# Where the filler stands beside the attention: first scores, changes of head, first scan products

## The chip, the cores and the metric

The kernel runs on one core of a Trainium2 chip, as one launch. The metric is the device time of that launch in microseconds, as the median of three runs. The core has five engines with a queue each: TensorE (PE; its weight loads are shown apart as PEld), VectorE (DVE), ScalarE (ACT), GpSimd (POOL) and SyncE (SP). SP computes nothing here; it issues nearly all the DMAs.

## The reference

One block of a diffusion backbone: 1024 latent tokens and 256 context tokens, width 1024, float32. What matters for the change is the token mixer, whose two halves don't depend on each other:

```python
hl = modulate(rmsnorm(xl, norm1_g), ...)        # (1024, 1024)
zl, xbcl, dtl, ql, kl, vl = split(hl @ w_in)    # one input projection
# attention half: 4 heads, two softmax maps each, over 256 + 1024 keys
w   = softmax(q1 k1) - lam * softmax(q2 k2)
o_l = rmsnorm(w @ v, subln_g) * (1 - lam_init)
# scan half: 16 heads in chunks of 128, forward and backward
ys_l = rmsnorm(ssd_bidir(xbcl, dtl, ...) * silu(zl), ssd_norm_g)
yl   = concat([ys_l, o_l]);  xl = xl + gate * (yl @ w_out)
```

Behind it come a gated feed-forward part with a convolution and a last norm, which the change doesn't touch.

## The kernel before, in words

The program goes through stages: start-up, input projection (`inproj`), the attention with filler, the rest of the scan, and `mixffn` (head norm, output projection, feed-forward). The change lies in the attention stage.

`attention` is a generator over 32 query tiles of 128 queries, n = 0 to 31, eight to a head. For each tile there are two groups of scores (c = 0 and 1, the two softmax maps): six products into one PSUM buffer `sc` of 1280 columns, which has no second copy, then the row maximum on DVE (`stat`), the exponential on ACT (`et`). `weigh` joins the two maps of the tile before on DVE, `transpose` brings the result into place in ten transposes (`tr`), and after every second tile `values` makes the product with V (`po`). In heads 0 and 1 the transposed weights are split into a high and a low part, in heads 2 and 3 not. At each new head `load_head` issues on SP's queue the loads of queries `S`, keys `K` (two maps, two parts, each twice) and values `V`; S and K have one buffer for each map and part in use, so that the new head's loads wait until the old head's last scores are through.

Where TensorE would wait, the generator yields a gap, a number in about microseconds, and `run` fills it: it adds `fill * gap` to a debt and takes steps from a second generator, the filler, until their stated costs have paid the debt. The filler is first `zproj`, the gate projection: eight units of weights, two halves of 512 tokens each, eight steps to a half, and each step three products `pz` at a cost of 0.65; behind each half come `zo` on ACT and DVE and a store to `zt`. When that is used up, the second `run` takes `ssd`, the scan: nine backward and two forward state steps (`s`, cost 3.4, with `xw` and `hb` or `H` multiplied on POOL), then eight chunks of outputs (`scs`, `yo`, `y`, `yt`), each with two halves, and seven more forward states. TensorE keeps the order in which all this is written (`pin`). What is left of the scan after the last tile runs beside the head norm (`cs_ps`, `cr_ps`, `bc_ps`), and then the output projection begins with the products `pw`. DMAs stand in SP's queue in one order, and one that waits holds up those behind it.

Of the kernel before, what the change touches and what calls it, by code (L numbers as in the profile page):

```python
# [75 lines left out]
E_S4 = "gvvv"  # L76
E_T4 = "vgvv"
E_W = "ggv"
FIRST_GAP = 12.0
S_BUFS = 6  # L80
D_BLOCKS = 3, 3, 3, 2
D_PLAIN = 2
# [13 lines left out]
B_FILL = 1.1  # L96
# [3 lines left out]
def r32(ap):  # L100
    return ap.bitcast(F32)


class Prog:
# [145 lines left out]
    def build(self):  # L250
        with ExitStack() as es:
            self.consts(es)
            hw, att, ssd = ExitStack(), ExitStack(), ExitStack()
            self.startup(hw)
            with ExitStack() as e:
                self.inproj(e, hw)
            e_pm, e_pa = ExitStack(), ExitStack()
            self.pm = self.pool(e_pm, "pm", 3, space=PSUM)
            self.pa = self.pool(e_pa, "pa", 2, space=PSUM)
            self.pin, self.rest = True, False  # L260
            at = self.attention(att)
            z = self.zproj(hw)
            self.run(at, z, A_FILL, False)
            hw.close()
            sd = self.ssd(ssd)
            self.run(at, sd, B_FILL, True)
            self.pin = False
            att.close()
            e_pa.close()

            def ssd_rest():
                self.rest = True
                for _ in sd:
                    pass
                ssd.close()

            with ExitStack() as e:
                self.mixffn(e, ssd_rest, e_pm)

    def run(self, at, filler, fill, drain):  # L280

        debt = 0.0
        for tile_no, gap in at:
            debt += fill * gap
            while debt > 0:
                cost = next(filler, None)
                if cost is None:
                    if not drain:
                        return
                    break  # L290
                debt -= cost
# [485 lines left out]
    def attention(self, es):  # L777

        nc = self.nc
        ap = self.pool(es, "ap", 2)  # L780
        heads = {}

        def load_head(h):
            pair, hh = divmod(h, 2)
            S, K = [], []
            for c in range(2):
                hc = 2 * hh + c
                s = ap.tile([P, SEQ], F32R, name="S")
                nc.sync.dma_start(r32(s), r32(self.qd[pair, hc].rearrange("a b r t -> (a b r) t")))
                k2 = []  # L790
                for part in range(2):
                    kt = ap.tile([P, TOK], F32R, name=f"K{part}")
                    for dup in range(2):
                        nc.sync.dma_start(r32(kt[dup * 64:(dup + 1) * 64, :]),
                                          r32(self.kd[pair, hc, part].rearrange("b r t -> (b r) t")))
                    k2.append(kt)
                S.append(s), K.append(k2)
            v = []
            for s in range(1 if h >= F32_FROM else 2):
                vt = ap.tile([P, NT, VD], F32R, name=f"V{s}")  # L800
                nc.sync.dma_start(r32(vt), r32(self.vd[h, s]))
                v.append(vt)
            return S, K, v

        def scores(n, c, st):
            h, qt = divmod(n, NL)
            S, K, _ = heads[h]
            sc = self.pa.tile([P, TOK], F32, tag="sc", name="sc", bufs=1)
            for o, w in ((0, 512), (512, 512), (1024, 256)):
                for i in range(2):  # L810
                    self.mm(sc[:, o:o + w], S[c][:, qt * P:(qt + 1) * P], K[c][i][:, o:o + w], i == 0, i == 1)
            et = ap.tile([P, TOK], F32, name="et", bufs=3)
            acc = self.s0[:, qt, h:h + 1] if c == 0 else st[:, 4:5]
            nc.vector.tensor_reduce(out=st[:, c:c + 1], in_=sc, axis=AX.X, op=ALU.max, negate=True)  # L814
            nc.scalar.activation(et, sc, AF.Exp, bias=st[:, c:c + 1], accum_out=acc)  # L815
            return et

        def weigh(n, st, ex):
            h, qt = divmod(n, NL)
            nc.vector.reciprocal(out=st[:, 5:6], in_=st[:, 4:5])  # L820
            nc.vector.scalar_tensor_tensor(out=st[:, 6:7], in0=st[:, 5:6], scalar=self.nlam[:, 0:1],
                                           in1=self.s0[:, qt, h:h + 1], op0=ALU.mult, op1=ALU.mult)
            nc.vector.scalar_tensor_tensor(out=ex[0], in0=ex[1], scalar=st[:, 6:7], in1=ex[0], op0=ALU.mult, op1=ALU.add)
            return ex[0]

        def transpose(n, w, wt, gi):
            m = 4 if gi < 2 else 2
            tr = self.pa.tile([P, 4, P], F32, tag="tr", name="tr")
            for i in range(m):
                kt = gi * 4 + i  # L830
                self.pe(nc.tensor.transpose(tr[:, i, :], w[:, kt * P:(kt + 1) * P], self.ident))
            qi = n % 2
            hi, lo = (t[:, :m, qi * P:(qi + 1) * P] for t in wt[gi])
            if n // NL >= F32_FROM:
                (nc.scalar.copy if WT_ENG[gi] == "a" else nc.vector.tensor_copy)(r32(hi), tr[:, :m, :])
            else:
                self.split(hi, lo, tr[:, :m, :])

        def values(n, wt):
            h, qt = divmod(n, NL)  # L840
            v = heads[h][2]
            po = self.pa.tile([P, 512], F32, tag="tr", name="po")
            for kt in range(NT):
                g, i = divmod(kt, 4)
                if h >= F32_FROM:
                    self.mm(po[:, :256], r32(v[0][:, kt, :]), r32(wt[g][0][:, i, :]), kt == 0, kt == NT - 1)
                    continue
                self.mm3(po[:, :256], (v[0][:, kt, :], v[1][:, kt, :]), (wt[g][0][:, i, :], wt[g][1][:, i, :]),
                         kt == 0, kt == NT - 1)
            oo = ap.tile([P, 256], F32, name="oo")  # L850
            nc.scalar.copy(oo, po[:, :256])
            nc.sync.dma_start(self.od[h][:, (qt - 1) * P:(qt + 1) * P], oo)

        n_all = DA_H * NL
        wt, done, prev = None, None, None
        for n in range(n_all + 2):
            if n < n_all:
                if n % NL == 0:
                    heads[n // NL] = load_head(n // NL)
                if n == 0:  # L860
                    yield n, FIRST_GAP
                st = ap.tile([P, 8], F32, name="stat", bufs=4)
                e0 = scores(n, 0, st)
            if done is not None:
                values(*done)
                done = None
                long = False
            else:
                long = True
                yield n, G_LONG if n < n_all else 2.0  # L870
            if prev is not None:
                m, pst, pex = prev
                w = weigh(m, pst, pex)
            if n < n_all:
                e1 = scores(n, 1, st)
            if prev is not None:
                if m % 2 == 0:
                    wt = [[ap.tile([P, 4, 256], F32R, name=f"wt{s}", bufs=4) for s in range(2)] for _ in range(3)]
                for gi in range(2):
                    transpose(m, w, wt, gi)  # L880
                yield n, G_A if long else G_B
                transpose(m, w, wt, 2)
                if m % 2 == 1:
                    done = (m, wt)
                yield n, G_A if long else G_B
            prev = (n, st, [e0, e1]) if n < n_all else None
# [749 lines left out]
```

## Time and profile before

| | before |
|---|---|
| median of three runs | 1842.23 us (1840.81 to 1844.36) |
| profiled execution, own time | 1847.34 us |
| its span | 1845.6 us |
| mean granted TensorE clock | 0.947 |
| PE, PEld, DVE, ACT, POOL busy | 87%, 69%, 67%, 41%, 59% of the span |
| first gate product to first product of the output projection | 430 to 909 us |

Times inside the program are microseconds from the start of the span. The busy shares are means over stages with different limits; products are pipelined, so that a busy PE isn't PE at its peak.

### The profile page before, as it was taken

To read this page: it belongs to the slowest core of one execution; us is meant where nothing else is said; L and a number is where in the kernel's file an instruction comes from. 1 tells how busy PE (TensorE), PEld (TensorE's weight loads), DVE (VectorE), ACT (ScalarE), POOL (GpSimd) and SP (SyncE) were. 2 spreads that over 40 slices of the span, in tenths; PEclk is the share of its full clock that TensorE was granted. 3 is DMA by queue.
4 is the path that set the end of the run, shared out by engine and by line. 5 is a ranking of instruction groups with operands and counts; after the bars stand their busy time and mean duration, and the time that the engine had idled before them with its cause. 6 is when DMAs were issued, how large, how long until landed. Compare 5 with 4: busy or idle time off the path is not lost.

```text
span 1845.6 us, 21271 instructions
## 1 busy us (share of the span) xinstructions
PE 1614.2 (87%) x7588; PEld 1274.8 (69%) x7588; DVE 1241.7 (67%) x1432; ACT 754.8 (41%) x1400; POOL 1096.5 (59%) x720
## 2 busy tenths in 40 slices
PE   5989989997899878898898967899999998989976
PEld 2687777885678656766577756677777776767755
DVE  4469843353556576887854686766767667898886
ACT  4433577632444333444443553233333334344242
POOL 3341587783010054677556768777887887777751
PEclk8899999998999998999999988899999999999988
DMA  7356766767241566546453312322222234743222
GB/s 270 126 183 207 266 205 231 250 216 206 100 120 44 144 221 190 173 152 213 135 202 120 121 45 74 108 86 86 97 90 100 86 106 166 265 162 126 63 78 91
DMA packets 138826, 273.35 MB, mean 148 GB/s; under 512 B 11984, under 2 KB 60544, under 8 KB 138208
## 3 DMA queue, kind: packets, MB, share of 16 engines
q1 hardware_dynamic: 138128, 271.03, 44.3%
q8 instruction: 60, 0.98, 0.2%
q0 software_dynamic: 592, 0.96, 0.2%
q14 instruction: 46, 0.38, 0.1%
HBM read 197.63 MB, written 74.32 MB: 147 GB/s over the span
## 4 chain that ended last, share of the span: by engine, by line
PE 37%; DVE 20%; POOL 18%; DMA 11%; issue 9%; ACT 4%; SPq 0%; POOLq 0%; DVEq 0%; ACTq 0%
PE pu L145 8%; POOL wlo L126 6%; PE pd L145 6%; POOL S L1206 4%; PE lat L145 4%; PE pz L145 3%; PE sc L145 3%; PE pb L145 3%; DMA K<-kd 3%; PE pw L145 3%; DVE T L126 2%; DMA gd<-R 2%; DMA wt<-wmB 2%; DVE jk L523 2%; PE pv L145 1%
## 5 line engine op out<-in xcount | busy, mean ns | idle before, releaser
L145 PE MATMUL pu<-T,whi 128*128 128x512 f32 x1232 | 389.9, 397 | 10.6 <-ACT whi L125 10.6
L145 PE MATMUL pu<-T,wlo 128*128 128x512 f32 x616 | 249.5, 405 | 38.6 <-POOL wlo L126 30.9
L145 PEld LDWEIGHTS pu<-T,whi 128*128 128x128 f32 x1232 | 236.9, 192 | 61.2 <-ACT whi L125 11.7
L126 POOL TENSOR_TENSOR wlo<-wraw,whi 128x512 fp32r<-128x512 f32 (+2 forms) x118 | 164.7, 1400 | 96.6 <-ACT whi L125 88.5
L145 PE MATMUL lat<-hl,w_hi 128*128 128x512 f32 x640 | 206.4, 399 | 5.0 <-DVE dtt L599 3.8
L145 PE MATMUL pd<-T,whi 128*128 128x512 f32 x560 | 182.3, 406 | 14.5 <-DVE T L126 8.1
L126 POOL TENSOR_TENSOR w_lo<-w_raw,w_hi 128x1024 fp32r<-128x1024 f32 (+1 forms) x36 | 83.7, 2328 | 184.6 <-ACT w_hi L125 162.9
L126 POOL TENSOR_TENSOR wlo<-S,whi 128x512 fp32r<-128x512 f32 (+2 forms) x122 | 169.0, 1395 | 27.0 <-ACT whi L125 26.7
L145 PEld LDWEIGHTS pu<-T,wlo 128*128 128x128 f32 x616 | 118.4, 192 | 80.0 <-POOL wlo L126 43.5
L814 DVE TENSOR_REDUCE stat<-sc 128x1 f32<-128x1280 f32 x64 | 95.3, 1488 | 109.1 <-PE sc L145 109.0
L125 ACT CAST whi<-wraw 128x512 fp32r<-128x512 f32 (+2 forms) x140 | 81.2, 581 | 194.9 <-PE pu L145 110.5
L145 PEld LDWEIGHTS lat<-hl,w_hi 128*128 128x128 f32 x640 | 123.0, 193 | 30.9 <-DVE dtt L599 4.0
L145 PE MATMUL sc<-K,S 128*128 128x512 f32 (+1 forms) x384 | 98.9, 395 | 49.5 <-DMA K<-kd 25.1
L125 ACT CAST whi<-S 128x512 fp32r<-128x512 f32 (+2 forms) x144 | 81.6, 571 | 147.6 <-PE pu L145 94.7
L815 ACT ACTIVATE et<-sc,stat 128x1280 f32<-128x1280 f32 x64 | 85.1, 1330 | 134.7 <-DVE stat L814 116.3
L145 PEld LDWEIGHTS pd<-T,whi 128*128 128x128 f32 x560 | 108.7, 196 | 43.9 <-DVE T L126 13.3
L145 PE MATMUL pd<-T,wlo 128*128 128x512 f32 x280 | 115.0, 411 | 16.7 <-POOL wlo L126 16.6
L145 PE MATMUL lat<-hl,w_lo 128*128 128x512 f32 x320 | 128.1, 400 | 0.0
L145 PEld LDWEIGHTS sc<-K,S 128*128 128x128 f32 x384 | 74.6, 203 | 77.1 <-ACT et L815 33.6
L538 POOL TENSOR_TENSOR R<-R,never 128x1024 f32<-128x1024 f32 x32 | 80.7, 2537 | 43.6 <-DMA R<-atd 41.6
L542 ACT ACTIVATE R<-R,lna 128x128 f32<-128x128 f32 x256 | 78.2, 391 | 56.0 <-POOL R L538 55.9
L908 POOL TENSOR_TENSOR xw<-xt,dte 128x1024 f32<-128x1024 f32 x18 | 36.9, 2050 | 96.1 <-DMA xt<-xtok 71.7
(283 smaller groups left out, 3729.9 us busy)
## 6 DMA issues: line engine op xcount, KB each, us to landing
wraw<-wUp SPq DMA_DIRECT2D x46, 512.0 KB, 3.3
wt<-wmB SPq DMA_DIRECT2D x32, 512.0 KB, 3.9
R<-atd SPq DMA_DIRECT2D x32, 512.0 KB, 5.5
stg<-gf_d SPq DMA_DIRECT2D x21, 768.0 KB, 4.9
w_raw<-wU SPq DMA_DIRECT2D x28, 512.0 KB, 5.0
gf_d<-T SPq DMA_DIRECT2D x11, 1024.0 KB, 4.2
K<-kd SPq DMA_DIRECT2D x32, 320.0 KB, 7.8
xt<-xtok SPq DMA_DIRECT2D x19, 512.0 KB, 5.2
```

Source lines behind the costliest of these rows:

```text
L125: nc.scalar.copy(hi, src)
L126: (lo_eng or nc.vector).tensor_tensor(out=lo, in0=src, in1=hi, op=ALU.subtract)
L145: self.pe(self.nc.tensor.matmul(out, lhsT=lhsT, rhs=rhs, start=start, stop=stop))
L523: nc.vector.scalar_tensor_tensor(out=jk, in0=wt, scalar=1.0, in1=scb, op0=ALU.mult, op1=ALU.mult, accum_out=self.modl[:, c:c + 1])
L538: nc.gpsimd.tensor_tensor(out=R[:, d], in0=R[:, d], in1=self.never[:, d].unsqueeze(1).broadcast_to([P, 8, P]), op=ALU.add)
L542: nc.scalar.activation(e, e, AF.Exp, bias=self.lna[:, d, i, h:h + 1], scale=1.0)
L814: nc.vector.tensor_reduce(out=st[:, c:c + 1], in_=sc, axis=AX.X, op=ALU.max, negate=True)
L815: nc.scalar.activation(et, sc, AF.Exp, bias=st[:, c:c + 1], accum_out=acc)
L908: nc.gpsimd.tensor_tensor(out=h3(xw), in0=h3(xt), in1=bc_h(self.dte, d, i), op=ALU.mult)
L1206: nc.gpsimd.tensor_tensor(out=t, in0=in0, in1=in1, op=op)
```

## The change

Three constants and the places where they act. The gap ahead of the first scores is 30 instead of 12. At the start of every later head there is a gap of 6, behind the issue of the head's loads and ahead of its first scores. The second `run`, the one with the scan as filler, starts with a debt of -8, so that the first 8 units of `fill * gap` bring no scan step.

```diff
-FIRST_GAP = 12.0
+FIRST_GAP = 30.0
+HEAD_GAP = 6.0
+SD_LAG = 8.0
...
-            self.run(at, sd, B_FILL, True)
+            self.run(at, sd, B_FILL, True, -SD_LAG)
...
-    def run(self, at, filler, fill, drain):
-
-        debt = 0.0
+    def run(self, at, filler, fill, drain, debt=0.0):
+
         for tile_no, gap in at:
             debt += fill * gap
             while debt > 0:
...
                 if n % NL == 0:
                     heads[n // NL] = load_head(n // NL)
-                if n == 0:
-                    yield n, FIRST_GAP
+                    yield n, HEAD_GAP if n else FIRST_GAP
                 st = ap.tile([P, 8], F32, name="stat", bufs=4)
                 e0 = scores(n, 0, st)
```

On TensorE 126 gate products instead of 51 stand ahead of the first scores, 33 instead of 9 between the last transposes of n=7 and the scores of n=8, and the last gate product stands in n=11 instead of n=16. The first state product stands in n=12 instead of n=16, the first chunk of outputs in n=18 instead of n=23. After the last scores (n=31) one chunk is left instead of four.

The first place is the ACT queue around the first exponentials (`et`). Before:

```order
L670 ACTIVATE rhi<-tm_3686 128x512
L772 ACTIVATE zo<-pz 128x512
L125 CAST w_hi<-w_raw 128x1024
L815 ACTIVATE et,s_95<-sc,stat 128x1280
L815 ACTIVATE et,stat<-sc,stat 128x1280
L815 ACTIVATE et,s_95<-sc,stat 128x1280
L772 ACTIVATE zo<-pz 128x512
```

Now:

```order
L671 ACTIVATE rhi<-tm_3686 128x512
L773 ACTIVATE zo<-pz 128x512
L127 CAST w_hi<-w_raw 128x1024
L773 ACTIVATE zo<-pz 128x512
L127 CAST w_hi<-w_raw 128x1024
L773 ACTIVATE zo<-pz 128x512 x2
L816 ACTIVATE et,s_95<-sc,stat 128x1280
```

Three more halves of the gate and the weights of one more unit (`w_hi`) stand ahead of the first exponential.

The second place is SP's queue around the keys of head 2 (`K` from `kd`). Before:

```order
L774 DMA zt<-zo 128x512
L794 DMA K_5242<-kd 64x1280
L789 DMA S<-qd 128x1024
L774 DMA zt<-zo 128x512
L794 DMA K_5242<-kd 64x1280
L794 DMA K_5245<-kd 64x1280 x2
L852 DMA od<-oo 128x256
L794 DMA K_5250<-kd 64x1280
L789 DMA S<-qd 128x1024
L794 DMA K_5250<-kd 64x1280
L794 DMA K_5253<-kd 64x1280 x2
L898 DMA xt<-xtok 128x1024
```

Now (`xt` and `btk` are inputs of a state step, `hbd` takes its result):

```order
L900 DMA btk<-btok 128x256
L795 DMA K_5334<-kd 64x1280
L790 DMA S<-qd 128x1024
L932 DMA hbd<-hb 128x1024
L795 DMA K_5334<-kd 64x1280
L795 DMA K_5337<-kd 64x1280 x2
L898 DMA xt<-xtok 128x1024
L853 DMA od<-oo 128x256
L795 DMA K_5342<-kd 64x1280
L790 DMA S<-qd 128x1024
L795 DMA K_5342<-kd 64x1280
L795 DMA K_5345<-kd 64x1280 x2
```

A store and a load of the scan, which waited behind all keys before, now stand between them.

The third place is the end of the attention, TensorE after the last scores. Before, of which the first rows:

```order
L831 MATMUL tr<-c_masks,et 128x128 x8
L1010 MATMUL yt<-c_masks,yg 128x128 x4
L831 MATMUL tr<-c_masks,et 128x128 x2
L145 MATMUL s<-xw,btk 128x512 x2
L145 MATMUL po<-wt_6667,V_5919 128x256 x4
L145 MATMUL po<-wt_6669,V_5919 128x256 x4
L145 MATMUL po<-wt_6671,V_5919 128x256 x2
L145 MATMUL scs<-cl,bl 128x128 x2
L145 MATMUL yo<-H_6803,cl 128x512
L145 MATMUL yo<-hb,cl 128x512
L145 MATMUL y<-xt,G 128x64 x8
L1010 MATMUL yt<-c_masks,yg 128x128 x4
```

Now, up to the output projection:

```order
L832 MATMUL tr<-c_masks,et 128x128 x8
L1010 MATMUL yt<-c_masks,yg 128x128 x8
L832 MATMUL tr<-c_masks,et 128x128 x2
L147 MATMUL po<-wt_6976,V_6184 128x256 x4
L147 MATMUL po<-wt_6978,V_6184 128x256 x4
L147 MATMUL po<-wt_6980,V_6184 128x256 x2
L189 MATMUL cs_ps<-sq,ones 32x512 x4
L147 MATMUL cr_ps<-gsel,part 128x4 x4
L147 MATMUL bc_ps<-dg,ones 128x512 x4
L189 MATMUL cs_ps<-sq,ones 32x512 x4
L147 MATMUL cr_ps<-gsel,part 128x4 x4
L147 MATMUL bc_ps<-dg,ones 128x512 x4
```

Nothing of the scan is left behind the last values, and the head norm stands alone. At the same place SP's queue has, before:

```order
L852 DMA od<-oo 128x256
L954 DMA bl<-bt 128x2x128
L1051 DMA o<-od 128x512 x8
L963 DMA G<-gd 128x1024
L133 DMA w_raw<-wO 128x512 x2
```

And now:

```order
L1098 DMA x_7153<-xT 128x1024
L1072 DMA yl<-yd 128x512 x2
L853 DMA od<-oo 128x256
L1098 DMA x_7153<-xT 128x1024
L1072 DMA yl<-yd 128x512
L1098 DMA x_7153<-xT 128x1024 x4
L1051 DMA o<-od 128x512 x8
L135 DMA w_raw<-wO 128x512 x2
```

Six loads of `x` and three of `yl`, which stood far behind, are now ahead of the loads of `o` for the head norm.

## Rows read from the trace of the kernel before

**Rows 1.** Busy time by stage: window, length, engines (instructions), clock, DMA share, GB/s

```profile
430.03:441.75 11.72, 11.72 (x52) 9.38 (x50) 8.55 (x10) 4.72 (x8) 8.28 (x5) 1.00 0.51 177
441.75:453.18 11.43, 0.00 (x1) 0.01 (x1) 0.67 (x1) 0.89 (x1) 2.34 (x1) 0.65 1.02 259
453.18:468.58 15.40, 8.14 (x28) 5.93 (x28) 3.01 (x3) 2.84 (x4) 0.00 (x0) 0.72 1.02 293
...
543.88:558.91 15.03, 12.21 (x48) 9.82 (x46) 6.52 (x11) 4.78 (x8) 0.00 (x0) 0.77 0.50 119
558.91:633.09 74.18, 72.22 (x420) 62.29 (x418) 48.90 (x63) 35.21 (x60) 3.29 (x1) 1.00 0.22 66
633.09:648.92 15.83, 8.52 (x30) 5.63 (x29) 5.89 (x8) 4.53 (x8) 3.90 (x3) 0.78 1.04 296
648.92:723.97 75.05, 58.95 (x243) 41.09 (x243) 54.01 (x57) 24.62 (x40) 41.78 (x22) 0.91 0.58 202
739.81:825.74 85.93, 77.07 (x413) 58.50 (x412) 69.58 (x68) 40.48 (x69) 60.01 (x45) 0.98 0.51 157
854.92:909.47 54.55, 44.69 (x217) 25.58 (x215) 48.16 (x67) 25.51 (x54) 38.67 (x27) 1.00 0.50 162
...
958.30:1062.34 104.04, 94.50 (x405) 75.27 (x406) 56.50 (x54) 41.82 (x72) 75.12 (x55) 0.98 0.37 122
980.00:1000.00 20.00, 15.27 (x62) 11.29 (x62) 9.55 (x10) 6.67 (x12) 13.63 (x11) 0.91 0.39 124
```

**Rows 2.** Chain of waits, 400 to 1000 us: start, length, what

```profile
443.10 8.19 DMA K<-kd
451.30 12.94 DMA K<-kd
...
540.97 10.81 DMA K<-kd
...
559.07 1.16 PE sc L145 x6
...
624.48 5.86 DMA K<-kd
630.36 12.86 DMA K<-kd
...
973.98 2.79 DMA yl<-yd
```

**Rows 3.** Costliest groups: row maximum and exponential

```profile
L814 DVE TENSOR_REDUCE stat<-sc 128x1 f32<-128x1280 f32 x64 | 95.3, 1488 | 109.1 <-PE sc L145 109.0
...
L815 ACT ACTIVATE et<-sc,stat 128x1280 f32<-128x1280 f32 x64 | 85.1, 1330 | 134.7 <-DVE stat L814 116.3
```

**Rows 4.** Weighing L823 (ns min/median/max), then timeline rows of DVE and POOL

```profile
L823 DVE SCALAR_TENSOR_TENSOR et<-et,stat x32: 1536/1552/3159, 469.0 to 841.9; 128x1280 f32<-128x1280 f32 x32
...
530.03 1.28 DVE L126 TENSOR_TENSOR wt<-tr,wt 128x512 fp32r<-128x512 f32 x2
...
663.87 3.16 DVE L823 SCALAR_TENSOR_TENSOR et<-et,stat 128x1280 f32<-128x1280 f32 x1
...
665.64 3.15 POOL L908 TENSOR_TENSOR xw<-xt,dte 128x1024 f32<-128x1024 f32 x1
```

**Rows 5.** Timeline after the last scores, PE and ACT: start, length, what

```profile
833.73 1.96 PE L145 MATMUL sc<-K,S 128*128 128x512 f32 x6 [2.22 <-ACT et L815]
...
843.95 1.89 PE L145 MATMUL y<-xt,G 128*128 128x64 f32 x16
...
850.40 4.48 PE L145 MATMUL po<-wt,V 128*128 128x256 f32 x20
...
861.73 1.26 ACT L182 ACTIVATE sq<-o 128x512 f32<-128x512 f32 x2 [4.87 <-DMA o<-od]
...
884.50 1.94 PE L145 MATMUL bc_ps<-dg,ones 128*128 128x512 f32 x4
...
909.47 0.76 PE L145 MATMUL pw<-yo,w_hi 128*128 128x512 f32 x1
```

## The prediction

> **What bounds the kernel now.** I read the sums by stage first [rows 1]. The change touches one stretch, from 430 us (first gate product pz) to 909 us (first product pw of the output projection); before 430 nothing moves. In that stretch three things set the pace in turn. First, TensorE stands still for keys: 0.00 of 11.43 us busy from 441.75 to 453.18, and 8.14 of 15.40 up to the start of query tile n=1 at 468.58, with DMA at 1.02. Second, in heads 0 and 1 TensorE itself is the bound: from n=9 to n=15, seven tiles in 74.18 us, 72.22 of them busy, 10.6 us a tile. Third, from n=16 on no engine is full: n=17 to 22 take 75.05 us (12.5 a tile) with TensorE at 58.95 and DVE at 54.01. There a score group waits for the row maximum and the exponential of the group before it, since the score bank has one buffer. The chain of waits [rows 2] shows where keys are late: 8.19 + 12.94 us at head 0, 10.81 at head 1, 5.86 + 12.86 at head 2. At the end, 54.55 us after the last value product are mostly scan: 44.69 us of TensorE, but only 25.58 of weight loads.
>
> **Edit 1, FIRST_GAP 12 to 30.** A gate step costs 0.65 in the planner's units, so the filler ahead of the first scores grows from 10.8/0.65, rounded up 17, to 27/0.65, 42 steps: 126 instead of 51 products. The 51 took 11.72 us [rows 1], 0.23 each, so 75 more take 17.2 us and end at 459.0. The first scores began at 453.18, when their first keys had come (443.10 + 8.19 and the hand-over); the second group of n=0 waited for keys until 464.24 (451.30 + 12.94) [rows 2], and n=1 began at 468.58. With the filler, the first scores end near 460.2, five gate steps (3.4 us) follow, and the second group still waits to 464.2. The key loads keep their place in the queue, and the weights of the third gate unit are loaded before them in both orders. So n=1 starts as before: cost 0, with 17.2 us of products done. If the cover failed (keys later by as much as the filler), it would cost up to 17; below 0 it can't go, the keys come no sooner.
>
> **Edit 2, HEAD_GAP 6.** At n=8, 5.4/0.65 gives 9 steps less the overshoot, in the order 8 more: 24 products, 5.5 us, between the last transposes of n=7 and the first scores of n=8. n=8 took 15.03 us against 10.6 for its neighbours [rows 1] because its second group waited for keys to 551.78 (540.97 + 10.81). Now its first group stands at 549.3 and the second at 554, after the keys. n=9 starts at 559.1 instead of 558.9. At n=16 and n=24 the gap holds scan steps.
>
> **What follows: the gate ends in n=11, not n=16.** 99 products are done early. n=9 to 11 take 3 x 10.6 less 2 (12 products fewer, and then the score chain: two groups of 1.2 for scores [rows 2], 1.49 for the maximum, 1.33 for the exponential [rows 3] and 0.5 of hand-overs make 9.0). n=12 starts at 588.9.
>
> **Edit 3, SD_LAG 8, and the scan in n=12 to 17.** The lag leaves 8/1.1 units of gap without filler, so n=12's first half has none: 9.5 us (9.0, and the weighing that delays a maximum). The eleven state steps then lie in n=12 to 17. Their price: n=17 to 22 held ten steps and took 12.5 a tile. In head 1 DVE also has the low parts of the transposed weights, 1.28 us a tile more [rows 4]; I put half on the path, 13.1 a tile. Bounds: 10.6 (the step is free) and 15.8 (n=16 before, key wait included). Five tiles make 65.5. The keys of head 2 cost n=16 some 5 us before (15.83 against 10.6); two extra state steps stand before them now, so I take 3 (bounds 0 and 19, the whole of 5.86 + 12.86). n=18 starts at 588.9 + 9.5 + 65.5 + 3 = 666.9.
>
> A row speaks against this part. The weighing (DVE, two inputs in SBUF) has a median of 1.55 us, but took 3.16 at 663.87, while on POOL a multiplication of the scan, begun at 665.64, took 3.15 [rows 4]. The scan now runs beside five more tiles.
> The Trainium skill says the same more strictly (SBUF — State Buffer, "Who interferes with whom"): a DVE instruction with two SBUF inputs and a GpSimd one that reads SBUF contend for one port pair, and the later one waits for the whole instruction. The trace agrees with 3.16 against 1.55. By that rule each tile in head 1 loses up to 1.6 us; by the average slot the loss is already inside the 12.5. It stands as a rival below.
>
> **n=18 to 30.** n=24 to 30, seven tiles with three and a half scan chunks, took 85.93 us, 12.28 a tile [rows 1]. Thirteen tiles make 159.6; seven chunks instead of six and a half add about 4. n=31 starts at 830.5, against 825.74 before: 4.8 later. Bounds: 10.6 a tile (22 us less) and 13.1 (11 more).
>
> **The tail.** Before, the last score group ended at 835.69 and pw began at 909.47 [rows 5], 73.8 us with more than three and a half chunks in it. After, only the last chunk is left. The same pieces up to the products y took 10 us (835.69 to 845.8); then come eight transposes, the second four of which wait for the chunk's last sum (three passes on POOL and two on DVE, estimated at 6 us, with the transposes 7), and the values, 4.5 [rows 5]: 21.6 us, so the last value product ends at 840.4 + 21.6 = 862.0. From there the head norm is bare: store, reload of o, squares, sums, broadcast, twice. Before, the first square began 6.8 us after the values (861.73) [rows 5]. Now six loads of x and three of yl, 3.9 MB, stand ahead of o in SP's queue; at the 293 GB/s of 453 to 468 us [rows 1] they need 13 us, begun some 2 before the values end, so the four o of the first half are in at 12 to 15. Each half then needs about 12, an estimate: sums and copy 2.5, root and reciprocal 2.5, four broadcasts (four rows of them took 1.94 [rows 5]) with scalings and splits 7. I take 37 for the whole, bounds 25 (no wait for the loads) and 54.6 (854.92 to 909.47, the same chain with the scan in it). pw begins at 899.0, 10.5 earlier.
>
> **Given back after it.** The squares and splits of yl for the mix fill that tail. From 980 to 1000 TensorE had 15.27 of 20 us, behind a wait of 2.79 for yl [rows 1, 2]; that is done now: 5 us less (bounds 0 and 8).
>
> Sum: -10.5 - 5 = -15.5 us against the profiled execution's own 1847.34 (span 1845.6), 1831.8. The runs' median lies 5.1 below that execution, so I predict 1827.
>
> **Rivals.** (A) The state steps are free in head 1, since its tiles have TensorE time to spare and the chain 9.0 hides them: 10.6 a tile, 12.5 less: 1814. For it: TensorE has 16 of 75 us idle there; against: DVE at 54.01 of 75.05. 17%. (B) The port pair decides: five weighings at +1.6 and the stretched POOL work behind the state chain, 8 to 13 more: 1835 to 1840. For it 3.16 against 1.55; against it the median, which most of the 32 weighings keep to, scan or not. 10%. (C) No change: the tail is a chain that only lay beside the scan; it keeps nearly its 54.6, 15 more: 1842. For it the loads now ahead of o, against it that those 54.6 hold 25 us of scan weights. 13%. (D) Slower: the loads of scan inputs and the stores of hb and yd now stand between the key loads of heads 2 and 3 in SP's one queue; each waits for its producer, and keys wait behind it. With the whole 18.7 us exposed at head 2 (instead of 3) and as much at head 3 (none before), 34 more: 1861; half of it gives 1844. It decides once the two together come 19 us late (a gain of 15.5 gone, and 0.2%). Against: between the first keys of head 2 stands one store, of a step whose products come before n=15's scores. 12%. That the change doesn't do what it says (first keys later by the filler's weights and stores) would bring 5 to 17 us back, 3%.
>
> **Numbers.** My forecast has 45%, from 1815 to 1838. 0.2%, 3.7 us, is about what can be told from no change (the runs lie within 3.6). Faster: 43 of the forecast's 45, A's 17, 5 of B, the last 3: 0.68. Same: 2 of the forecast, 5 of B, 9 of C, 2 of D: 0.18. Slower: 4 of C, 10 of D: 0.14. The range leaves out the best end (A with a short tail) and D in full: 1809 to 1847.
>
> **What would show it.** In the profile after: no idle TensorE between 430 and 459, n=1 still near 468.6; n=9 near 559; the last gate product near 588 and the first state product near 596; n=18 near 667 and n=31 near 830; only one chunk after the last scores, values ended near 862, pw near 899; then 90 to 100 us for the mix instead of 104. I am wrong if n=31 starts after 845, if scores at n=16 or 24 wait over 10 us for keys, or if pw starts over 45 us after the last value product.

## The result, and the profile after

The changed kernel took 1893.34 us (median of 4 runs, 1887.28 to 1901.74) against 1841.52 for the kernel before (4 runs): a ratio of 1.027, 95% interval 1.0244 to 1.0295. It is slower by 2.7%, where 1827 was predicted. The profiled execution took 1887.28 us, with a span of 1885.5 us. Its gate products begin at 426.10 us, 3.9 earlier than before, so times below are best compared from that point.

The sums by stage, as in [rows 1] (window, length, busy us with instructions of PE, PEld, DVE, ACT and POOL, clock, DMA share, GB/s). The cuts are the starts of the first scores of n=0, 1, 8, 9, 12, 16, 18, 24, 31; the last window runs from the last value product to the first pw.

```profile
426.10:454.69 28.59, 28.59 (x128) 23.66 (x126) 9.91 (x11) 7.28 (x10) 13.09 (x7) 1.00 0.81 223
454.69:473.11 18.42, 7.25 (x29) 5.46 (x27) 4.20 (x5) 3.93 (x6) 0.00 (x0) 0.69 0.74 267
473.11:553.25 80.14, 78.06 (x416) 65.50 (x417) 50.80 (x66) 37.19 (x62) 7.60 (x3) 0.97 0.27 76
553.25:562.31 9.06, 9.06 (x47) 7.30 (x46) 4.86 (x6) 4.62 (x8) 0.00 (x0) 1.00 0.22 71
562.31:593.31 31.00, 29.72 (x175) 24.98 (x175) 20.21 (x27) 14.29 (x26) 0.00 (x0) 1.00 0.21 69
593.31:650.55 57.24, 40.44 (x176) 28.91 (x177) 41.29 (x49) 18.15 (x32) 28.19 (x13) 0.87 0.75 234
650.55:679.70 29.15, 22.41 (x92) 15.90 (x91) 17.67 (x21) 8.47 (x14) 14.54 (x10) 0.79 0.70 247
679.70:774.32 94.62, 77.09 (x388) 58.53 (x387) 72.90 (x66) 36.67 (x63) 66.47 (x39) 0.93 0.53 156
774.32:872.62 98.30, 80.78 (x410) 60.34 (x408) 65.70 (x70) 40.59 (x69) 59.69 (x46) 0.94 0.41 125
903.94:952.76 48.82, 22.16 (x48) 7.63 (x48) 26.62 (x52) 33.22 (x65) 16.52 (x12) 0.69 0.64 216
```

Four things are to be seen. The first window has no idle TensorE, as wanted, but the second is 18.42 us against 15.40 before, with TensorE busy 7.25. n=8 fell from 15.03 to 9.06, but n=7, at whose end the gap stands, rose from 11.45 to 16.77. The stretch from n=18 to n=31 takes 192.9 us, 14.8 a tile, where TensorE is busy for 157.9. And the 48.82 us of the tail hold only 22.16 us of TensorE, at a granted clock of 0.69; before they held 44.69 of 54.55.

Against the forecast, each stage counted from its own start (the difference of the last column adds up to 59.2; less the 3.9 us by which this execution reached the gate earlier it is, to 0.2, what separates 1887.3 from 1831.8):

| stage | forecast | after | excess |
|---|---|---|---|
| first gate product to n=12 | 158.9 | 167.2 | 8.3 |
| n=12 to n=18 | 78.0 | 86.4 | 8.4 |
| n=18 to n=31 | 163.6 | 192.9 | 29.3 |
| n=31 to pw | 68.5 | 80.1 | 11.6 |
| pw to the end | 931.1 | 932.7 | 1.6 |

**The start.** Groups of waits between 426 and 473 us (engine, line, what it waited for; us, times, longest), and one row of the chain of waits:

```profile
ACT zo L773 <- DMA zt<-zo: 13.6, 1, 13.6
PE sc L147 <- ACT et L816: 8.1, 1, 8.1
```

```profile
451.04 11.57 DMA zt<-zo
```

The second scores of n=0 no longer wait for keys. They wait for the exponentials of the first, which stand in ScalarE's queue behind a gate copy. That copy needs a buffer whose store was issued at 451.04, behind eight key and two value loads, and took 11.57 us to land. The longer filler makes more gate outputs before the first scores than the two buffers hold.

**An even tile of head 3.** TensorE's timeline from the first scores of n=26 to those of n=27 (start, us, what, with the idle time before it and what ended it):

```profile
803.30 1.72 PE L147 MATMUL sc<-K,S 128*128 128x512 f32 x6
804.85 1.02 PE L147 MATMUL yo<-hb,cl 128*128 128x512 f32 x2
805.71 1.90 PE L147 MATMUL y<-xt,G 128*128 128x64 f32 x16
809.94 1.09 PE L1010 MATMUL yt<-c_masks,yg 128*128 128x128 f32 x4 [2.33 <-DVE yg L999]
810.82 3.04 PE L147 MATMUL s<-xw,btk 128*128 128x512 f32 x4
813.30 1.72 PE L147 MATMUL sc<-K,S 128*128 128x512 f32 x6
814.85 1.03 PE L832 MATMUL tr<-c_masks,et 128*128 128x128 f32 x8
816.13 0.44 PE L832 MATMUL tr<-c_masks,et 128*128 128x128 f32 x2 [0.24 <-ACT wt L836]
818.11 0.74 PE L147 MATMUL sc<-K,S 128*128 128x512 f32 x2 [1.55 <-ACT et L816]
```

Between the first scores and the second lie 10.00 us, filled with scan. In them is a wait of 2.33 for sums of y and, behind it, products that take longer: the granted clock was 0.98 from 803.30 to 809.94 and 0.52, TensorE's lower level of 1.2 GHz, from 809.94 to 813.30. The four transposes and four s there took 1.09 and 3.04, where the same rows in the run without head gaps, shown below, took 0.60 and 2.02 at 1.00. So about 3.8 us of the 10.00 are the wait and the lower clock, the rest is products. Between the second scores and the next first ones only ten transposes of weights stand, and TensorE waits 1.55 us for the exponential all the same: 4.81 us. This is the shape of n=24, 28 and 30 too.

**A gap.** TensorE in the gap ahead of n=24, from the second scores of n=23:

```profile
756.40 1.43 PE L147 MATMUL sc<-K,S 128*128 128x512 f32 x6 [0.81 <-ACT et L816]
...
767.28 1.98 PE L147 MATMUL y<-xt,G 128*128 128x64 f32 x16
772.52 1.09 PE L1010 MATMUL yt<-c_masks,yg 128*128 128x128 f32 x4 [3.26 <-DVE yg L999]
773.40 1.91 PE L147 MATMUL yo<-H,cl 128*128 128x512 f32 x2
774.32 1.41 PE L147 MATMUL sc<-K,S 128*128 128x512 f32 x1
```

17.92 us pass between the two score groups, none of it for keys; TensorE is busy in 14.35 of them. The gap at n=16 took 10.85 (639.70 to 650.55), with three state steps in it and a wait for the sum of one of them:

```profile
649.47 2.07 PE L147 MATMUL s<-xw,btk 128*128 128x512 f32 x2 [2.68 <-DVE hb L922]
```

The chain of waits has one load of keys there, landed at 643.10, and runs on through a store of the scan's state behind it, whose buffer the next state step needs. That store landed at 653.81, so it holds up a step in n=16 and not the scores at 650.55:

```profile
637.40 5.70 DMA K<-kd
...
645.02 8.79 DMA hbd<-hb
```

The scores of heads 2 and 3 wait for no key in this trace.

**The tail.** From the chain of waits behind the last value product:

```profile
908.01 7.77 DMA o<-od
...
936.71 2.53 DMA yl<-yd
```

Five x loads and one of yl are issued between the store of the last output and the reload of o; the reload takes 7.77 us. Later the chain runs through loads of yl for the mix, ahead of the second half of the head norm. The weighing of [rows 4] has the same median as before, and 9 of the 32 lasted over 2 us, against 10 before, so the shared port (rival B) isn't where the change lost its time:

```profile
L824 DVE SCALAR_TENSOR_TENSOR et<-et,stat x32: 1543/1552/3158, 473.5 to 884.7; 128x1280 f32<-128x1280 f32 x32
```

### The profile page after: what moved, and what is told of

Read it like the earlier page. It is cut to its first block, busy times and chain, and to the rows that moved or that the text cites. A ratio compares the mean times of both kernels' runs of the same rounds, so it can differ in the third digit from the quotient of the medians.

```text
span 1885.5 us, 21279 instructions
## 1 busy us (share of the span) xinstructions
PE 1626.4 (86%) x7588; PEld 1281.2 (68%) x7588; DVE 1223.4 (65%) x1426; ACT 758.9 (40%) x1406; POOL 1109.4 (59%) x726
## 4 chain that ended last, share of the span: by engine, by line
PE 36%; POOL 19%; DVE 18%; issue 10%; DMA 9%; ACT 6%; SPq 1%; POOLq 0%; ACTq 0%; DVEq 0%
PE pu L147 7%; POOL wlo L128 7%; PE pd L147 5%; PE lat L147 4%; POOL S L1206 4%; PE pb L147 3%; PE sc L147 3%; PE pz L147 3%; PE pw L147 2%; PE po L147 2%; DVE T L128 2%; DMA wt<-wmB 2%; DVE jk L524 2%; DVE stat L815 2%; ACT et L816 2%
## 5 line engine op out<-in xcount | busy, mean ns | idle before, releaser
L147 PE MATMUL pu<-T,whi 128*128 128x512 f32 x1232 | 390.9, 398 | 10.6 <-ACT whi L127 10.6
L147 PEld LDWEIGHTS pd<-T,whi 128*128 128x128 f32 x560 | 108.0, 194 | 44.2 <-DVE T L128 12.3
L147 PE MATMUL sc<-K,S 128*128 128x512 f32 (+1 forms) x384 | 102.7, 406 | 37.7 <-ACT et L816 37.5
```

The source lines that it names most:

```text
L147: self.pe(self.nc.tensor.matmul(out, lhsT=lhsT, rhs=rhs, start=start, stop=stop))
```

## Experiments

The theories: **places** (what a piece of scan costs depends on which of the intervals between score groups it stands in), **amount** (scan inside the attention costs more than it saves later), **gap** (filled changes of head cost by themselves), and for the ends, the queues named above. The constants of the changed kernel are FIRST_GAP 30, HEAD_GAP 6, SD_LAG 8; a diff below is against it.

### Each edit alone, and one pair

```diff
-HEAD_GAP = 6.0
-SD_LAG = 8.0
+HEAD_GAP = 0.0
+SD_LAG = 0.0
```

> FIRST_GAP 30 alone, head gap and lag at zero. In TensorE's order the scan then begins four tiles earlier than before, at exactly the places between the score groups that it had before (y, its weights and the output product behind the odd tile, the rest behind the next first scores). Placement theory (the lag and the gaps moved the scan's pieces to places where scores wait for them): n=18 to 30 at 12 to 13 us a tile as before, first scores of n=31 at 828 to 842, total 1825 to 1842. Amount theory (scan inside the attention costs more than it saves in the tail, wherever it stands): n=18 to 30 at 14 to 15 us a tile as in the changed kernel, n=31 after 855, total 1865 to 1885. On both the tail (last scores to the first mix product) shows whether two chunks left instead of five shorten it: my prediction's 59 us, the changed kernel's 74.

Measured: 1839.42 us, ratio to before 1.0003 (0.9980 to 1.0026). n=25 to n=31 took 78.8 us, 13.1 a tile, n=31 began at 842.9, the tail from n=31 to pw lasted 64.6 (the profiled execution was the slowest of ten, 10 us above the median). No change in the total: the amount theory's 1865 to 1885 fails (the scan begins four tiles earlier, and no 30 us are lost), the total lies in the range of places.

```diff
-FIRST_GAP = 30.0
-SD_LAG = 8.0
+FIRST_GAP = 12.0
+SD_LAG = 0.0
```

> HEAD_GAP 6 alone, first gap 12 and no lag. The gap at n=8 holds gate products, the gap at n=16 two state steps in a row (8 us of them stood alone in the changed kernel), the gap at n=24 a whole chunk of scan (n=23 lasted 24.5 us there, tiles about it 14). Placement theory: the gaps at n=16 and n=24 cost 7 to 10 us each, the places behind n=24 are those of before and cost nothing, the tail has two chunks less: total 1842 to 1858, with n=23 over 20 us and n=25 to 30 at 12 to 13. Amount theory: only about two chunks more than before stand inside the attention, a quarter or a third of what the changed kernel moved: total 1848 to 1860 with the excess spread over n=20 to 30.

Measured: 1856.56 us, 1.0116 (1.0083 to 1.0149). n=15 lasted 28.4 us, n=23 24.4, n=26 to 30 12.6 a tile. The price lies in the two gaps and the tiles beside them, as the places theory had it, though the gap at n=16 cost more than the 7 to 10 I gave it. 8 us of it are a wait of another kind, for a load of scan input that was issued behind the keys in SP's one queue:

```profile
642.55 3.75 PE L147 MATMUL s<-xw,btk 128*128 128x512 f32 x4 [7.99 <-DMA btk<-btok]
```

```diff
-FIRST_GAP = 30.0
-HEAD_GAP = 6.0
+FIRST_GAP = 12.0
+HEAD_GAP = 0.0
```

> SD_LAG 8 alone. Less scan stands inside the attention than before, and from n=24 on in the other places: the transposes of a chunk and the state steps of the next stand between the first and the second scores of the even tiles, the weights and first output product between the second scores and the transposes. Placement theory: n=24 to 30 cost 1 to 2 us a tile more than before, and the tail has about one chunk more: total 1850 to 1868. Amount theory: less scan inside is cheaper, n=31 starts at or before 826, the tail takes a few us more: total 1836 to 1848.

Measured: 1845.06 us, 1.0043 (1.0025 to 1.0061). n=24 to n=30 took 89.8 us, 12.8 a tile, but 11.8 from n=26 on: the places of the lag that I had called worse are the best seen. What was lost came in the tail, 70.2 us from the values to pw. My reading of these places was wrong, and the total lies in the amount theory's range (1836 to 1848), so this run alone speaks for amount.

```diff
-HEAD_GAP = 6.0
+HEAD_GAP = 0.0
```

> FIRST_GAP 30 and SD_LAG 8 without the head gaps: the changed kernel without its second edit. The places of the lag (as in the run with the lag alone) now hold from n=20 to n=31. Placement theory: 1 to 2 us a tile over twelve tiles against the run with FIRST_GAP alone, so 12 to 24 us above that run, 1845 to 1865; against the changed kernel 25 to 40 us less, of which the two gaps with scan in them are 15 to 20. Amount theory: within 5 us of the run with FIRST_GAP alone or below it, both at 1860 to 1885.

Measured: 1827.56 us, 0.9938 (0.9913 to 0.9963): faster than before, and 61 us below the changed kernel by the ratios (0.0332 of 1841). Against the changed kernel the direction of places held, its price list (1845 to 1865) didn't. Against the run with FIRST_GAP 30 alone the order is that of amount: one chunk less inside the attention, 12 us less. Its stages from n=12 to n=31:

```profile
597.13:639.37 42.24, 33.83 (x177) 25.48 (x176) 29.91 (x40) 17.81 (x31) 13.97 (x7) 0.96 0.72 229
639.37:668.85 29.48, 21.99 (x88) 14.70 (x87) 18.84 (x22) 8.46 (x14) 12.46 (x7) 0.71 0.74 228
668.85:744.83 75.98, 63.98 (x310) 46.81 (x309) 58.97 (x60) 30.45 (x51) 49.37 (x30) 0.96 0.53 165
744.83:829.02 84.19, 76.06 (x400) 56.70 (x400) 66.26 (x67) 40.13 (x69) 60.97 (x43) 0.98 0.57 179
```

Thirteen tiles take 160.2 us, 12.3 each. From its profile (1401.2 us from the first gate product to the end, 1459.4 in the changed kernel) the 58.2 us split into -2.3 up to n=12, 14.7 for n=12 to 17, 32.8 for n=18 to 30 (10.6 of it in n=23), 11.6 from n=31 to pw and 1.4 behind. Not all of the 32.8 is places: the changed kernel has seven chunks ahead of n=31 and this one five, and from n=18 to n=24, where its 88 products more stand, TensorE is busy 14.7 us longer. The tail gives nothing back for them: values to pw took 42.2 us here with three chunks left, 37.9 in the run with lag 0 with two, 48.8 in the changed kernel with one. The same even tile here:

```profile
771.04 1.41 PE L147 MATMUL sc<-K,S 128*128 128x512 f32 x6
772.28 0.60 PE L1010 MATMUL yt<-c_masks,yg 128*128 128x128 f32 x4
772.72 2.02 PE L147 MATMUL s<-xw,btk 128*128 128x512 f32 x4
775.48 1.43 PE L147 MATMUL sc<-K,S 128*128 128x512 f32 x6 [0.74 <-ACT et L816]
...
777.62 0.61 PE L147 MATMUL scs<-cl,bl 128*128 128x128 f32 x4
778.07 1.02 PE L147 MATMUL yo<-H,cl 128*128 128x512 f32 x2
...
780.76 0.50 PE L147 MATMUL sc<-K,S 128*128 128x512 f32 x1 [0.59 <-ACT et L816]
```

The two intervals take 4.44 and 5.28 us. In both TensorE ends up waiting for the exponential, so the scan in them is free.

### The places without the gaps

```diff
-HEAD_GAP = 6.0
-SD_LAG = 8.0
+HEAD_GAP = 0.0
+SD_LAG = -1.0
```

> FIRST_GAP 30, no head gaps, SD_LAG -1: from n=20 to n=31 TensorE's order holds the scan's pieces at exactly the places that the changed kernel has from n=24 on (after the first scores of an even tile: the last output product, y, its transposes and the next state steps; behind its second scores nothing but the transposes of the weights), with no gap filled at a change of head. Places theory (these places are what costs): even tiles 14 to 15 us, odd 12.8 to 13.5 as in the changed kernel, so about 2 us a tile over twelve tiles above the run with FIRST_GAP 30 and lag 8 (12.1 to 12.3 a tile): total 1845 to 1862. Gap theory (the places are harmless, the gaps leave the scan's other engines behind and the scores pay for it afterwards): 12 to 12.6 us a tile, total 1825 to 1840. The tail has two chunks left: 57 to 62 us from the last scores to the first mix product if the scan left over is what fills it, 75 if not.

Measured: 1861.23 us, 1.0115 (1.0086 to 1.0143), 33 us by the ratios above the run with FIRST_GAP 30 and lag 8. n=20 to n=31 took 160.0 us, 14.5 a tile, against 135.3. The even tile n=26 repeats the changed kernel's, wait included:

```profile
783.46 1.90 PE L147 MATMUL y<-xt,G 128*128 128x64 f32 x16
787.68 1.09 PE L1010 MATMUL yt<-c_masks,yg 128*128 128x128 f32 x4 [2.33 <-DVE yg L999]
788.56 2.94 PE L147 MATMUL s<-xw,btk 128*128 128x512 f32 x4
```

So these places and one chunk more, with no gap filled, cost about half of the 61 us that lie between the run without gaps and the changed kernel. What the places cost at equal amount is shown against the run with lag 0, which has no head gaps and two chunks left too. From n=18 to n=31 TensorE has 749 products here and 747 there, and takes 184.7 us against 169.1; one unit of lag makes 21 us by the ratios. The changed kernel and the run with FIRST_GAP 30 and lag 8 have the same scan from n=25 to n=31, where the changed kernel is 10.5 us slower (82.11 against 71.56, rows as in [rows 1]):

```profile
790.51:872.62 82.11, 69.33 (x360) 52.72 (x360) 57.40 (x61) 34.92 (x60) 44.56 (x33) 0.96 0.33 103
757.46:829.02 71.56, 66.19 (x361) 50.05 (x361) 58.41 (x60) 35.21 (x61) 51.84 (x36) 1.00 0.50 158
```

3.1 us of that are longer busy time, at a clock of 0.96 against 1.00, and 7.4 are idle time. With two chunks left, values to pw took 37.9 us, the tail the prediction had.

### The gaps without the places

The gap at n=8 alone, the scan's places in the second half held:

```diff
-SD_LAG = 8.0
+SD_LAG = 14.6
...
-                    yield n, HEAD_GAP if n else FIRST_GAP
+                    yield n, (FIRST_GAP, HEAD_GAP, 0.0, 0.0)[n // NL]
```

> FIRST_GAP 30, the gap of 6 at n=8 alone, none at n=16 and n=24, and the lag set to 14.6 to hold back the 6.6 us by which the scan would begin earlier: its places from n=21 to n=31 and the scan left for the tail are those of the run with FIRST_GAP 30 and lag 8. My prediction's step (5.5 us of gate products done in a wait for keys): 4 to 6 us below that run, total 1820 to 1826. Its rival (TensorE's wait there has other work behind it anyway): within 2 us of it, 1826 to 1830.

Measured: 1834.47 us, 0.9974 (0.9957 to 0.9992), not below the run without it but 7 us above. The wait at n=8 did go: n=9 began at the same distance, 136.5 us, from the first gate product in both, with 24 gate products more done. But n=12 to n=15 then took 46.9 us instead of 42.2: n=12, with no gate products left in it, lasted 13.15 instead of 8.87, so these products had been free where they were. In it the second scores wait for the exponential:

```profile
603.01 2.50 PE L147 MATMUL sc<-K,S 128*128 128x512 f32 x6 [6.13 <-ACT et L816]
```

The first scores had ended at 596.88, but their row maximum stood in VectorE's queue behind the weighing of n=11 and began at 600.02; the granted clock of the tile was 0.74, against 1.00. In the run without the gap, gate products held the scores back until the weighing was through. Four more us went in n=21. The rival is nearer than my step, and neither had the sign.

All three gaps, with the scan of n=25 to n=31 and of the tail as in the run without gaps:

```diff
-SD_LAG = 8.0
+SD_LAG = 27.8
```

> All three head gaps as in the changed kernel, but the lag at 27.8, so that n=25 to n=31 and the tail hold exactly the scan of the run with FIRST_GAP 30 and lag 8, at its places. What is left of the loss is then the gaps at n=16 (state steps) and n=24 (a chunk) themselves. Gap price alone: n=15 about 9 and n=23 about 10 us longer than in that run, less what is done before (fewer state steps in n=12 to 15, 5 us of gate products at n=8): total 1832 to 1845, n=25 to 30 at 12 to 12.5 a tile. If a gap also leaves the chain of the scan behind for the tiles after it, n=25 to 30 stay at 14: total 1850 to 1865.

Measured: 1840.1 us, 1.0007 (0.9986 to 1.0028), 13 us above the run without gaps. n=25 to n=31 took 73.0 us, 12.2 a tile: the gap leaves nothing behind for the tiles after it. n=22 and n=23 took 16.7 and 22.1 us against 10.95 and 13.94; the gap at n=16, with four state products in it, cost 1.

### The output reload ahead of the loads for the mix

```diff
-                nc.sync.dma_start(os[t][h], self.od[h][:, sls[t]])
+                last_o = nc.sync.dma_start(os[t][h], self.od[h][:, sls[t]])
...
-                nc.sync.dma_start(y, self.yd[k][:, sls[t]])
+                with self.tc.issue_after(last_o.ins):
+                    nc.sync.dma_start(y, self.yd[k][:, sls[t]])
...
-            nc.sync.dma_start(x1[:, dt, :], io["xT"][:, dt, :])
+            with self.tc.issue_after(last_o.ins):
+                nc.sync.dma_start(x1[:, dt, :], io["xT"][:, dt, :])
```

> The changed kernel with one order on SP's queue: the loads of y and x for the mix stage are issued only behind the eight loads of the attention's output (TensorE's order is untouched). There the output loads waited 3.1 us behind four x and one y load and took 7.8 us, and ScalarE and VectorE worked on y ahead of the head norm. Queue theory of the tail: from the last value product to the first mix product 36 to 42 us in place of 49, total 8 to 13 us below the changed kernel (1880 to 1886). Bare norm theory (the steps of the head norm are a chain of one engine after the other, whatever else is in the queue): 46 to 49 us, total 1889 to 1894.

Measured: 1881.01 us, 1.0216 (1.0190 to 1.0242), 10 us below the changed kernel by the ratios. Values to pw took 40.8 us in place of 48.8. In its chain of waits the reload is shorter, and no load of yl is left:

```profile
908.58 4.77 DMA o<-od
```

The queue theory of the tail holds; the edit moves the loads of x and yl together, so what each of them cost is not shown.

### Half a microsecond of lag

```diff
-SD_LAG = 8.0
+SD_LAG = 8.5
```

> The changed kernel with the lag at 8.5 in place of 8, nothing else. In TensorE's order half a us of planned cost is enough: from n=24 on the scan's pieces stand again at the places of the kernel before (output products, y and transposes behind the first scores of an even tile, one state step behind its second scores, a chunk's start and first y behind the odd tile), while all gaps and all but half a us of the scan inside the attention stay. Places theory: n=25 to 30 at 12.3 to 13 us a tile in place of 13.7, so 4 to 8 us there, and a few us more or less in n=18 to 23, where the places are new (a transpose moved from the even tile's second scores to the odd tile's): total 1876 to 1889. Amount or gap theory (what is inside the attention costs, wherever it stands): 1890 to 1896.

Measured: 1893.28 us, 1.0276 (1.0249 to 1.0304): no change in the total, against my forecast. The stretch that was to change did: n=25 to n=31 took 74.4 us instead of 82.1, with this shape at n=26 (second scores at 819.35, 6.23 us after the first):

```profile
818.94 0.66 PE L1010 MATMUL yt<-c_masks,yg 128*128 128x128 f32 x4 [0.87 <-DVE yg L999]
819.35 1.41 PE L147 MATMUL sc<-K,S 128*128 128x512 f32 x6
```

The 7.7 us were lost again around it: 3.1 in n=18 to 24, 3.1 from n=31 to pw, and 7.8 behind pw, where no kernel here differs in its work (this execution was the slowest of its four, 5.4 us above their median). That last stage took 930 to 934 us in nine of the traces after the change and 938 to 941 in three, with 936.1 before; what moves it stays open. So this run confirms places in its stretch and does not confirm them in the total.

### Fewer gate products ahead of the first scores

```diff
-FIRST_GAP = 30.0
-HEAD_GAP = 6.0
-SD_LAG = 8.0
+FIRST_GAP = 22.0
+HEAD_GAP = 0.0
+SD_LAG = -3.0
```

> FIRST_GAP 22 in place of 30, no head gaps, lag -3: TensorE's order is that of the run with FIRST_GAP 30 and lag 8 from n=15 on to the end, but 93 gate products stand ahead of the first scores in place of 126; the other 33 follow in n=12 to 14. In the changed kernel the first scores came 5.4 us later than the keys allowed (28.6 us after the first gate product; 23.2 in the kernel before), and the exponentials of the first scores waited in ScalarE's queue behind a gate copy whose buffer came free only when a store landed behind the key and value loads (13.6 us). With 93 products that copy, the fourth, stands behind the first scores. Store theory: n=0 at 23 us and n=1 at 38 to 40 after the first gate product (28.6 and 47.1 there), the 7.5 us of products cost 2 to 4 us later: 3 to 6 us below the run with FIRST_GAP 30 and lag 8, total 1821 to 1825. Rival (each gate product ahead of the keys is worth its time, and the exponentials wait for something else): n=1 at 45 or later, total 1828 to 1834.

Measured: 1829.14 us, 0.9919 (0.9891 to 0.9947); by the ratios level with the run with FIRST_GAP 30 and lag 8 (0.9938), both faster than before. n=0 began 21.5 us after the first gate product and n=1 38.2 (28.6 and 47.0 there). ScalarE has the exponential ahead of the copy now:

```profile
454.13 1.33 ACT L816 ACTIVATE et<-sc,stat 128x1280 f32<-128x1280 f32 x1
...
462.97 0.60 ACT L773 ACTIVATE zo<-pz 128x512 f32<-128x512 f32 x1 [7.42 <-DMA zt<-zo]
```

The store theory holds for the start. Of the 8.8 us, n=12 to n=15 took 7.4 back, more than the 2 to 4 I had written. n=31 stood 4.6 earlier in the profiled execution, whose stage behind pw was of the long kind (938.5); the ratios put it 3.5 us below the run with FIRST_GAP 30 and lag 8, with intervals that overlap, so a gain in the total is not shown.

### The transposes of y one unit later

```diff
-LAG = 1
-Z_BUFS = 2
+LAG = 2
+Z_BUFS = 3
...
-                yg = sp.tile([P, 512], F32, name="yg")
+                yg = sp.tile([P, 512], F32, name="yg", bufs=3)
```

> The changed kernel with the transposes of a y taken one more unit later (LAG 2, a third buffer for yg and zc): from n=24 to n=30 TensorE's order is word for word that of the changed kernel, but the four transposes right behind the products y are those of the unit before, whose sums on GpSimd and VectorE are long done. It tells apart what costs in an even tile there, 10.0 us from its first to its second scores at n=26 (5.5 to 6 us of products at full clock, and 2.3 us of wait for yg in front of the transposes). Chain theory (TensorE waits in its fixed order for the sums of the y it has just made, and runs at half clock behind the wait): that stretch falls to 6 to 7.5 us, n=25 to 31 takes 74 to 77 us in place of 82.1, total 1875 to 1886. Crowding theory (too many products stand between two score groups, whatever they wait for): 8.5 to 10 us as before, n=25 to 31 at 79 to 82, total 1888 to 1895.

Measured: 1887.71 us, 1.0246 (1.0212 to 1.0279), not told apart from the changed kernel. n=25 to n=31 took 84.5 us. The transposes no longer wait, but the state products behind them do:

```profile
803.23 0.60 PE L1010 MATMUL yt<-c_masks,yg 128*128 128x128 f32 x4
805.62 1.12 PE L147 MATMUL s<-xw,btk 128*128 128x512 f32 x2 [1.79 <-DVE yg L999]
806.95 1.61 PE L147 MATMUL s<-xw,btk 128*128 128x512 f32 x2 [0.20 <-ACT yt L1013]
```

The chain theory's 74 to 77 us fail. The kernel gives y, yt and s the same three PSUM buffers, and the waits of the s, for what VectorE and ScalarE read out of y and yt, fit a product that comes third and finds none free. Behind them the second scores took 3.12 us at a granted clock of 0.50. So the wait moved instead of going, which fits crowding of the interval; no run here takes the wait, the lower clock and the number of products apart.

### The intervals side by side

From the starts of the score rows: first to second scores + second to next first, for the even tile n=26 and the odd n=27, and the six tiles from n=25 to n=31, in which all of them have the same scan (the one with lag -1 one product group scs more).

| kernel | n=26 | n=27 | n=25 to n=31 |
|---|---|---|---|
| before | 6.22 + 4.50 | 8.00 + 8.29 | 75.0 |
| changed | 10.00 + 4.81 | 6.19 + 7.31 | 82.1 |
| no head gaps | 4.44 + 5.28 | 6.45 + 7.96 | 71.6 |
| no head gaps, lag -1 | 9.89 + 4.81 | 6.25 + 7.33 | 87.3 |
| all gaps, lag 27.8 | 4.45 + 6.28 | 6.12 + 7.96 | 73.0 |
| lag 8.5 | 6.23 + 4.50 | 7.98 + 6.76 | 74.4 |
| transposes later | 8.50 + 6.21 | 7.03 + 7.38 | 84.5 |

No interval of these is under 4.4 us: the scores, their row maximum, the exponential and the hand-overs, about half of the 9.0 that the prediction had for both groups. Scan that fits into that is free; what is over it lengthens the interval, in the changed kernel with waits and a lower clock on top, and what an interval leaves unused is no use to its neighbour. The changed kernel puts 10.00 us in one interval and leaves the next at its floor.

## Why the prediction was wrong

- **n=18 to 30, "12.28 a tile": the step that failed**, with 29.3 of 59.2 us: 14.8 a tile were measured. I took the average of the old n=24 to 30 for a price of the scan. It was the price of one arrangement. The head gaps add 6.6 units of debt at n=16 and 24 (at n=8 they pay for gate products, and the scan begins that much earlier) and shift every piece after them; the lag of 8 takes one part back. Without the head gaps n=18 to n=30 took 12.3 a tile, with five chunks ahead of n=31 in place of seven; in the changed kernel's places, without gaps and with six, 14.5 from n=20 on. With the same scan, n=25 to n=31 took 13.7 a tile in the changed kernel and 11.9 in the run without head gaps. The order of both kernels was there to be read, and I counted its pieces without asking which interval each stood in.
- **"At n=16 and n=24 the gap holds scan steps": priced at nothing beyond them.** n=23 lasted 24.49 us against 13.94 without the gap, n=15 20.77 against 12.15, and no key was late there. A chunk started in a gap has no score work beside it: at n=24 its products took 14.35 us and its waits the rest of 17.92.
- **n=12 to 17, 13.1 a tile: 8.4 us short.** n=15, with the gap at n=16, is 7.7 over its 13.1, n=12 4.2 over its 9.5; without the gaps these six tiles took 71.7 us, less than the 78.0 forecast. It is what stands in the gap: with all gaps and the lag at 27.8 they took 72.3.
- **Edit 1, cost 0: 7.1 us too little up to n=9.** Key order and key times were right, but I followed the filler on TensorE and in the weight loads alone, not its copies on ScalarE and their stores behind the keys.
- **Edit 2 at n=8 was right where I looked** (n=1 to n=9 took 89.2 us, 90.5 forecast; 89.5 in the run without the gap), but the products it brought forward had been free in n=12.
- **The tail, 37 us: 48.8.** I did have loads ahead of o, but let the norm follow undisturbed. yl work in ScalarE's and VectorE's queues and the reload at 7.77 us made 8 of the 11.8; with o first it is 40.8, inside the prediction's bounds of 25 to 54.6. The step also paid for a tail with one chunk left, but three left had taken 42.2 and two 37.9: the last chunks lie beside the head norm almost for nothing. Rival C named this end.
- **Rivals.** None had the mechanism. D (keys late at heads 2 and 3 behind the scan's stores) had the sign, but no score waits for keys there; where the queue shows, it is the other way round, a state store of 8.79 us behind the keys. B fails by the weighing, which is over 2 us in 9 of 32 tiles, as it was in 10 before. The wrong-if line on n=31 (after 845) and that on pw (over 45 us) both came true.

What stays open: how the 61 us add up exactly (at equal amount of scan, places 21 and gaps 13; the reload's order 10, by ratios from different kernels; what the two chunks more cost was not run alone), why the run with lag 8.5 gained 7.7 us in its stretch and nothing in the total, and the late stage that varies by some 8 us.

## What to carry to other kernels

Where two pieces of work alternate through one buffer, the unit of account is the interval between them, not the tile: in these runs filler was free up to the interval's floor and cost its time or more above it, and a constant that moves filler by half an interval can turn one into the other. Before taking a mean from a trace as a price, look in the new order whether the same pieces stand in the same intervals. And follow filler to the end of its own chain, copies, buffers and stores, through every queue it shares with what it fills in for.

## What the runs showed that was not expected

- Less filler did not make two tiles shorter: n=11 and n=12 took 22.7 us in the run with the gap at n=8 and 20.0 in the one without, which has 24 gate products more in them. The row of the 6.13 us wait shows where it went: scores that came earlier queued for their row maximum behind the weighing.
- A store issued while the key and value loads ran took 11.57 us to land, against 2.9 for the shortest of the same five.
- Behind a wait of 2.33 us four state products took 3.04 us in place of 2.02, and four transposes 1.09 in place of 0.60: part of the wait is paid again in the rows that follow it, at a granted clock of 0.52. Over n=24 to 30 the clock was 0.94, and 0.98 in the run without head gaps.
